# Casting and subtracting streamed weights two k-tiles at a time, with two S5 phase tables in a shared buffer

## The chip, the cores and the metric

The kernel runs on one core of one Trainium2 chip. The metric is device time in microseconds (us); three timed runs of a version give a median. The core's engines named below are PE (TensorE, the matmuls), PEld (the weight load of PE), DVE (VectorE), ACT (ScalarE) and SP (SyncE, which issues most of the loads). Each engine takes its instructions in a fixed order, and they wait for one another by semaphores.

## What is computed

The reference is one pre-norm layer of a hybrid encoder on 256 tokens of 2048 channels, in float32. Cut to what matters here:

```python
h = rmsnorm(x, norm_mix_g)
proj = h @ w_in                        # 2048 x 12288
lru_x, lru_gate, q, k, v, ssm_u, gates = split(proj)
y_a = rg_lru_branch(lru_x, lru_gate, ...)
y_b = chunk_attention_branch(q, k, v, rel_bias)
y_c = gelu(s5_branch(ssm_u, ...))      # complex diagonal state space
br_a, br_b = y_a @ w_branch[0], y_b @ w_branch[1]
br_c = (y_c @ w_branch[2]) * sigmoid(y_c @ ssm_w_glu)
g = sigmoid(gates + gate_bias)
x = x + (g[0] * br_a + g[1] * br_b + g[2] * br_c) @ w_out
h = rmsnorm(x, norm_ffn_g)
x = x + (silu(h @ w_ffn_gate) * (h @ w_ffn_up)) @ w_ffn_down   # hidden 5632
out = rmsnorm(x, norm_final_g)
```

The S5 branch turns each state by an angle per token: `lb = mag * (cos(ang) + i sin(ang))`. The kernel runs the recurrence with real factors `mag` and multiplies by tables of cosine and sine before and after it; the argument of these tables is the phase that the change speaks of.

## The kernel before

**Weight stream.** Every large matrix is cut into columns of 512 and rows of 128 (a k-tile). `add_job` (L161) queues a block of 512 columns as steps of `UK = 2` k-tiles; a step is called a unit here. `load_unit` (L166) brings a unit into a `raw` tile of 2 x 512 columns by one DMA from SP (L170; the first two units use two DMAs, L175), and then, k-tile by k-tile, calls `split` (L120): ACT casts the raw weights to fp32r into `hi` (L123), DVE subtracts `hi` from the raw weights into `lo` (L124). There are 3 `raw` buffers (of a unit each) and `HBUF = 7` buffers each of `hi` and `lo` (of a k-tile each). A `raw` buffer is free for the next DMA when its two subtractions are done; a `hi` or `lo` buffer is free for the next k-tile when its matmuls are done. The last 512 columns are special: eight units are cast into large tiles that stay (`resident`, L908, through `place`, L916).

**Matmuls.** The tokens, split in the same way, are the stationary operand, the weights move. `as_body` (L185) does three matmuls per k-tile and half of the tokens: high by `hi` (L198), high by `lo` (L199), low by `hi` (L200). That makes 12 matmuls per unit, which add up in PSUM until the block's last unit; then `evac` takes the sum out.

**Order.** `run_steps` (L209) writes out the steps; loads and splits are written `LOOK` = 2 units ahead and with a raised priority. Behind each step the generators of the three mixers (`gen_lru`, `gen_att`, `gen_s5`) get a share of instructions (`bg_mix`, L772). A scheduler that simulates a timeline then fixes the order of instructions on each engine, under these priorities and the buffers that are free. So a changed length or buffer can change the order of anything.

**Stages.** Mixer projections, gates and branch products come first, with the mixers' own arithmetic beside them; `drain("s5")` and `gen_yc` (L757) stand before the first product of the S5 output. Then the output projection, the FFN in two parts, and the last 512 columns with the final norm (`last_body`, L944; `finish`, L920).

**S5 phase tables.** `gen_s5` works through 8 blocks of channels with two halves each (`sb`, L696). For each half, `q` and `w` (L698, L699, one buffer each, tags `sq` and `sw`) are filled: `q` on ACT (L702), `w` and again `q` on DVE (L703, L704), `w` on ACT (L705). Sine of `q` and cosine of `w` (L706, L707) make the tables `sn` and `cs_`, which have one buffer each too. The products with the matmul results (L720 to L723) go into `ma` and `mb` (L717, tags `sA` and `sB`, one buffer each); sums, scans and further products follow, and L738 is the last to read `mb`. The matmuls L745 and L746 read `ma`, and L748 puts their result into `u`.

Of the kernel before, what the change touches and what calls it, by code (L numbers as in the profile page):

```python
# [10 lines left out]
F32 = mybir.dt.float32  # L11
F32R = mybir.dt.float32r
# [6 lines left out]
P = 128  # L19
S = 256  # L20
D = 2048
# [10 lines left out]
HBUF = 7  # L32
# [13 lines left out]
# columns of the constant array  # L46
# [8 lines left out]
# rows of the per-channel parameter block  # L55
# [5 lines left out]
def trunk(  # L61
# [21 lines left out]
    # ---------------------------------------------------------------- inputs  # L83
# [6 lines left out]
    # the tensor engine's clock rises while the first loads are under way  # L90
# [17 lines left out]
    def load_params():  # L108
        act.dma_start(cst[:, P:], consts[:, P:])
        prm_r = const.tile([P, P], F32, name="prm_r")  # L110
        act.dma_start(prm_r[R_G2:R_G2 + 16], norm_ffn_g[0].rearrange("(k p) -> k p", p=P))
        act.dma_start(prm_r[R_CW:R_CW + 32], lru_conv_w[0].rearrange("c (k p) -> (c k) p", p=P))
        for r0, src in ((R_CB, lru_conv_b), (R_BA, lru_ba), (R_BX, lru_bx), (R_LAM, lru_lambda), (R_D, ssm_d)):
            act.dma_start(prm_r[r0:r0 + 8], src[0].rearrange("(k p) -> k p", p=P))
        tps = sm("prm_ps")
        pe.transpose(tps[:, :R_N], prm_r[:R_N, :], ident[:R_N, :R_N])
        vec.tensor_copy(prm, tps[:, :R_N])

    # ---------------------------------------------------------------- helpers
    def split(dst_hi, dst_lo, src, scale=None):  # L120
        """src (optionally scaled per partition) as an exact sum of two f32r parts"""
        if scale is None:
            act.copy(dst_hi, src)  # L123
            vec.tensor_sub(dst_lo, src, dst_hi.bitcast(F32))  # L124
        else:
            act.activation(dst_hi, src, AF.Identity, scale=scale)
            vec.scalar_tensor_tensor(dst_lo, src, scale, dst_hi.bitcast(F32), ALU.mult, ALU.subtract)

    def rstd_of(dst, ss, scr):
        """dst = (ss / D + EPS) ** -0.5 on [P, 2] tiles, refined by a Newton step"""  # L130
        v, t = scr[:, 0:2], scr[:, 2:4]
        vec.tensor_scalar(v, ss, 1.0 / D, EPS, ALU.mult, ALU.add)
        act.activation(t, v, AF.Sqrt)
        vec.reciprocal(dst, t)
        vec.tensor_mul(t, dst, dst)
        vec.tensor_mul(t, t, v)
        vec.tensor_scalar(t, t, -0.5, 1.5, ALU.mult, ALU.add)
        vec.tensor_mul(dst, dst, t)

    def expacc(dst, src, pool, tag):  # L140
        """dst = exp(src) in float32 accuracy"""
# [16 lines left out]
    # ---------------------------------------------------------------- main stream of weight units  # L158
    steps = []

    def add_job(src, kt, c0, body, pre=None):  # L161
        """columns c0..c0+512 of a [kt * 128, n] matrix, UK k-tiles at a time"""
        for k0 in range(0, kt, UK):
            steps.append((src, k0, c0, body, kt, pre if k0 == 0 else None))

    def load_unit(st, idx):  # L166
        src, k0, c0, _, _, _ = st
        raw = wp.tile([P, UK, 512], F32, tag="raw", name="raw", bufs=3)
        if idx > 1:
            nc.sync.dma_start(  # L170
                raw, src[k0 * P:(k0 + UK) * P, c0:c0 + 512].rearrange("(k p) n -> p k n", p=P))
        parts = []
        for kk in range(UK):
            if idx <= 1:
                nc.sync.dma_start(raw[:, kk, :], src[(k0 + kk) * P:(k0 + kk + 1) * P, c0:c0 + 512])  # L175
            if idx in place:
                hi, lo = place[idx](kk)
            else:
                hi = wp.tile([P, 512], F32R, tag="hi", name="hi", bufs=HBUF)
                lo = wp.tile([P, 512], F32R, tag="lo", name="lo", bufs=HBUF)  # L180
            split(hi, lo, raw[:, kk, :])
            parts.append((hi, lo))
        return parts

    def as_body(get_x, evac):  # L185
        """out tiles: tokens stationary, weights moving"""
# [22 lines left out]
    def run_steps(bg, budget):  # L209
        """emits every queued step; background work fills in behind each"""  # L210
# [21 lines left out]
    # ---------------------------------------------------------------- x^T and its norm  # L232
# [3 lines left out]
    def transpose_tokens(src, kt0, name):  # L236
        """two 128-column tiles of token-major src, transposed into one PSUM bank [P, 2, S]"""
        t = sm(name)
        for i in range(2):
            for h in range(2):  # L240
                pe.transpose(t[:, i * S + h * P:i * S + (h + 1) * P], src(h, kt0 + i), ident)  # L241
        return t
# [31 lines left out]
    # ---------------------------------------------------------------- projections of the mixers  # L274
    # token-major input of the S5, replaced by its feature-major output block by block
# [8 lines left out]
    def fm_evac(name, dst):  # L284
        """scales by rstd and transposes; dst(m) is the place of feature tiles m, m + 1"""
# [21 lines left out]
    # RG-LRU  # L307
# [18 lines left out]
    # gates  # L326
# [69 lines left out]
    # attention  # L396
# [26 lines left out]
    # ---------------------------------------------------------------- background: RG-LRU  # L423
    def gen_lru():
        # softplus(-lambda)
# [20 lines left out]
        for hf in range(2):  # L446
# [40 lines left out]
            # t1 = tanh(L / 2), t3 = 1 / (1 + t1) refined; t1 := -(1 - a) / 2  # L487
# [26 lines left out]
    # ---------------------------------------------------------------- background: attention  # L514
# [72 lines left out]
    # ---------------------------------------------------------------- background: S5  # L587
    def gen_s5():
        # per-state parameters, state = 128 * j + partition
# [20 lines left out]
        # f = angle / (2 pi), reduced to [-0.5, 0.5]  # L610
# [42 lines left out]
        for b in range(8):  # L653
# [18 lines left out]
            # partitions 32 * jj.. hold the channels of state tile 4 * b + jj: B (re, im), then u, as hi and lo  # L672
# [8 lines left out]
            # stationaries [B_hi; B_hi; B_lo] and moving parts [u_hi; u_lo; u_hi], 32 channels each  # L681
# [14 lines left out]
            for sb in range(2):  # L696
                j0 = 4 * b + 2 * sb
                q = mx.tile([P, 2, S], F32, tag="sq", name="sq")  # L698
                w = mx.tile([P, 2, S], F32, tag="sw", name="sw")  # L699
# [72 lines left out]
    def bg_mix(budget):  # L772
        """spends the budget of a unit on background steps; a negative cost ends the generator's turn"""
# [41 lines left out]
    # ---------------------------------------------------------------- output projection  # L815
# [30 lines left out]
    # ---------------------------------------------------------------- FFN  # L846
# [53 lines left out]
    # ---------------------------------------------------------------- last columns and the final norm  # L900
    # the weights of the last 512 columns stay on chip, so that the first 128 tokens finish early
# [6 lines left out]
    def resident(i, kk):  # L908
        q = i // n_res
        if i % n_res == 0 and kk == 0:  # L910
            pool, tags = ((big, ("TH", "TL")), (fp, ("h2h", "h2l")))[q]
            held.append(tuple(pool.tile([P, 8, 512], F32R, tag=t, name="res") for t in tags))
        return tuple(t[:, (i % n_res) * UK + kk, :] for t in held[q])

    for i in range(2 * n_res):
        place[base + i] = lambda kk, i=i: resident(i, kk)  # L916
# [86 lines left out]
```

## Time and profile before

| what | value |
|---|---|
| timed runs | 1636.93, 1636.76, 1635.12 us, median 1636.76 us |
| profiled execution, from its first to its last instruction | 1637.8 us (the page gives no other time for it) |
| PE / DVE / ACT busy, share of the span | 98% / 68% / 58% |
| casts `hi<-raw` (L123) | 1088 of 128x512, 621 ns mean |
| subtractions `lo<-raw,hi` (L124) | 1088 of 128x512, 688 ns mean |
| unit loads of 512 KB | median 3.7 to 4.7 us from issue to landing, by matrix |
| HBM rate over the span | 185 GB/s |

The busy time of PE counts overlapping matmuls as one stretch, and the end of a matmul is modelled, so 98% says that PE seldom stood empty, not that each matmul came as early as it could. The distance from one matmul's start to the next one's tells the latter. A row of the timeline gives the start, the duration, the engine, the line, the operation, output and inputs, the number of instructions merged into the row, and in square brackets the idle time before it with what ended it.

### The profile page before, as it was taken

To read this page: it belongs to the slowest core of one execution; us is meant where nothing else is said; L and a number is where in the kernel's file an instruction comes from. 1 tells how busy PE (TensorE), PEld (TensorE's weight loads), DVE (VectorE), ACT (ScalarE), POOL (GpSimd) and SP (SyncE) were. 2 spreads that over 40 slices of the span, in tenths; PEclk is the share of its full clock that TensorE was granted. 3 is DMA by queue.
4 is the path that set the end of the run, shared out by engine and by line. 5 is a ranking of instruction groups with operands and counts; after the bars stand their busy time and mean duration, and the time that the engine had idled before them with its cause. 6 is when DMAs were issued, how large, how long until landed. Compare 5 with 4: busy or idle time off the path is not lost.

```text
span 1637.8 us, 21032 instructions
## 1 busy us (share of the span) xinstructions
PE 1612.1 (98%) x7263; PEld 1307.1 (80%) x7263; DVE 1111.4 (68%) x1910; ACT 951.6 (58%) x1696; POOL 0.8 (0%) x6
## 2 busy tenths in 40 slices
PE   7999999999999999999999999999999999999997
PEld 4877877778888777778888888888888888888886
DVE  4869889879697978876666555555555555555654
ACT  4677677675768676665455554555444455455443
POOL 0000000000000000000000000000000000000000
PEclk9999999999999999999999999999999999999999
DMA  8665566655554646565666666666666666666564
GB/s 224 198 178 150 166 183 185 186 165 174 165 177 146 197 152 214 170 201 185 214 236 182 193 191 190 185 192 190 187 192 196 193 187 194 190 192 186 188 191 144
DMA packets 169933, 304.21 MB, mean 186 GB/s; under 512 B 22185, under 2 KB 26721, under 8 KB 169057
## 3 DMA queue, kind: packets, MB, share of 16 engines
q1 hardware_dynamic: 153104, 292.66, 59.5%
q10 hardware_dynamic: 16720, 10.20, 2.3%
q8 instruction: 57, 0.93, 0.2%
q14 instruction: 52, 0.42, 0.1%
HBM read 300.71 MB, written 2.11 MB: 185 GB/s over the span
## 4 chain that ended last, share of the span: by engine, by line
PE 86%; DVE 5%; ACT 3%; DMA 3%; issue 2%; ACTq 0%; DVEq 0%
PE mm L199 27%; PE mm L200 27%; PE mm L198 27%; DMA raw<-in_w_in 3%; DVE lo L124 2%; ACT hi L123 1%; PE y_ps L746 1%; PE mm L957 1%; PE at_ps L241 1%; PE mm L956 1%; PE mm L958 1%; PE y_ps L745 0%; ACT bc L691 0%; DVE xc L470 0%; ACT bc L692 0%
## 5 line engine op out<-in xcount | busy, mean ns | idle before, releaser
L124 DVE TENSOR_TENSOR lo<-raw,hi 128x512 fp32r<-128x512 f32 x1088 | 736.9, 688 | 441.6 <-ACT hi L123 438.9
L123 ACT CAST hi<-raw 128x512 fp32r<-128x512 f32 x1088 | 658.7, 621 | 611.9 <-DVE lo L124 322.2
L199 PE MATMUL mm<-lo,xth 128*128 128x512 f32 x768 | 304.8, 397 | 2.6 <-DVE lo L124 2.6
L200 PE MATMUL mm<-hi,xtl 128*128 128x512 f32 x768 | 302.7, 394 | 0.0
L198 PE MATMUL mm<-hi,xth 128*128 128x512 f32 x768 | 284.2, 396 | 9.6 <-ACT hi L123 9.6
L200 PE MATMUL mm<-hi,h2l 128*128 128x512 f32 x704 | 275.0, 391 | 0.0
L198 PE MATMUL mm<-hi,h2h 128*128 128x512 f32 x704 | 274.9, 390 | 0.0
L199 PE MATMUL mm<-lo,h2h 128*128 128x512 f32 x704 | 274.0, 389 | 0.0
L198 PEld LDWEIGHTS mm<-hi,xth 128*128 128x128 f32 x768 | 144.0, 189 | 46.5 <-ACT hi L123 13.7
L199 PEld LDWEIGHTS mm<-lo,xth 128*128 128x128 f32 x768 | 145.0, 189 | 39.5 <-DVE lo L124 8.3
L200 PEld LDWEIGHTS mm<-hi,xtl 128*128 128x128 f32 x768 | 145.2, 189 | 29.4 <-issue 0.4
L199 PEld LDWEIGHTS mm<-lo,h2h 128*128 128x128 f32 x704 | 132.2, 188 | 27.3
L200 PEld LDWEIGHTS mm<-hi,h2l 128*128 128x128 f32 x704 | 132.1, 188 | 27.2
L198 PEld LDWEIGHTS mm<-hi,h2h 128*128 128x128 f32 x704 | 132.2, 188 | 26.8
L198 PE MATMUL mm<-hi,at 128*128 128x512 f32 x312 | 121.6, 390 | 0.0
L200 PE MATMUL mm<-hi,at 128*128 128x512 f32 x312 | 121.6, 390 | 0.0
L199 PE MATMUL mm<-lo,at 128*128 128x512 f32 x312 | 121.4, 389 | 0.0
L199 PEld LDWEIGHTS mm<-lo,at 128*128 128x128 f32 x312 | 58.6, 188 | 12.2
L200 PEld LDWEIGHTS mm<-hi,at 128*128 128x128 f32 x312 | 58.6, 188 | 12.2
L198 PEld LDWEIGHTS mm<-hi,at 128*128 128x128 f32 x312 | 58.6, 188 | 11.9
L200 PE MATMUL mm<-hi,mtl 128*128 128x512 f32 x128 | 50.3, 393 | 0.0
L199 PE MATMUL mm<-lo,yc 128*128 128x512 f32 x128 | 50.1, 391 | 0.0
(312 smaller groups left out, 1624.7 us busy)
## 6 DMA issues: line engine op xcount, KB each, us to landing
raw<-in_w_in SPq DMA_DIRECT2D x190, 512.0 KB, 4.2
raw<-in_w_ffn_gate SPq DMA_DIRECT2D x88, 512.0 KB, 4.0
raw<-in_w_ffn_up SPq DMA_DIRECT2D x88, 512.0 KB, 3.7
raw<-in_w_ffn_down SPq DMA_DIRECT2D x88, 512.0 KB, 4.7
raw<-in_w_branch SPq DMA_DIRECT2D x48, 512.0 KB, 4.1
raw<-in_w_out SPq DMA_DIRECT2D x32, 512.0 KB, 4.6
raw<-in_ssm_w_glu SPq DMA_DIRECT2D x16, 512.0 KB, 4.7
xa<-in_x SPq DMA_DIRECT2D x8, 256.0 KB, 3.8
```

What stands on the lines that cost most here:

```text
L123: act.copy(dst_hi, src)
L124: vec.tensor_sub(dst_lo, src, dst_hi.bitcast(F32))
L198: pe.matmul(acc[h], xh[:, k, hs], hi, start=k == 0, stop=False)
L199: pe.matmul(acc[h], xh[:, k, hs], lo, start=False, stop=False)
L200: pe.matmul(acc[h], xl[:, k, hs], hi, start=False, stop=k == kt - 1)
L241: pe.transpose(t[:, i * S + h * P:i * S + (h + 1) * P], src(h, kt0 + i), ident)
L746: pe.matmul(yp[rs, :S], ct[:, 1, rs], m2[:, i, :], start=False, stop=True)
L956: pe.matmul(last_acc[h], ah[:, k, hs], hi, start=k == 0, stop=False)
L957: pe.matmul(last_acc[h], ah[:, k, hs], lo, start=False, stop=False)
L958: pe.matmul(last_acc[h], al[:, k, hs], hi, start=False, stop=k == kt - 1)
```

## The change

It makes the unit the grain of the split as well as of the load. `hi` and `lo` become tiles of 2 x 512 columns with four buffers each, so that eight k-tiles of each part have room in place of seven, given back two at a time. From the third unit on, one cast and one subtraction on 1024 columns take the place of two and two on 512; the first two units are still loaded and split by k-tile. The resident tiles of the last columns are handed out by unit, and are split in the same way. The matmuls, their order in a step and the loads are as before.

The room for the eighth k-tile comes from the S5: `q` and `w` are now the two halves of one tile `qw` that has the tag `sB`, that is, the single buffer in which `mb` lies. In program order that buffer goes to `qw` of a half, then to `mb` of that half, then to `qw` of the next half; each must wait until the last reader of the one before is done.

The raw block of per-channel parameters, `prm_r` (L110), moves from a buffer of its own into the S5's tag `uf` (a tile that each S5 block fills at L677 and reads at L748). It is loaded at the start and transposed once (L116); the profile has that transpose at 35.5 us and the first use of `uf` by the S5 at 82.7 us.

The rest of the diff takes out comments and is left out.

```diff
-HBUF = 7
+HBUF = 4
...
-        prm_r = const.tile([P, P], F32, name="prm_r")
+        prm_r = mx.tile([P, S], F32, tag="uf", name="prm_r")[:, :P]
...
     def load_unit(st, idx):
         src, k0, c0, _, _, _ = st
         raw = wp.tile([P, UK, 512], F32, tag="raw", name="raw", bufs=3)
+        if idx in place:
+            hi, lo = place[idx]()
+        else:
+            hi = wp.tile([P, UK, 512], F32R, tag="hi", name="hi", bufs=HBUF)
+            lo = wp.tile([P, UK, 512], F32R, tag="lo", name="lo", bufs=HBUF)
         if idx > 1:
             nc.sync.dma_start(
                 raw, src[k0 * P:(k0 + UK) * P, c0:c0 + 512].rearrange("(k p) n -> p k n", p=P))
-        parts = []
-        for kk in range(UK):
-            if idx <= 1:
+            split(hi, lo, raw)
+        else:
+            for kk in range(UK):
                 nc.sync.dma_start(raw[:, kk, :], src[(k0 + kk) * P:(k0 + kk + 1) * P, c0:c0 + 512])
-            if idx in place:
-                hi, lo = place[idx](kk)
-            else:
-                hi = wp.tile([P, 512], F32R, tag="hi", name="hi", bufs=HBUF)
-                lo = wp.tile([P, 512], F32R, tag="lo", name="lo", bufs=HBUF)
-            split(hi, lo, raw[:, kk, :])
-            parts.append((hi, lo))
-        return parts
+                split(hi[:, kk, :], lo[:, kk, :], raw[:, kk, :])
+        return [(hi[:, kk, :], lo[:, kk, :]) for kk in range(UK)]
...
             for sb in range(2):
                 j0 = 4 * b + 2 * sb
-                q = mx.tile([P, 2, S], F32, tag="sq", name="sq")
-                w = mx.tile([P, 2, S], F32, tag="sw", name="sw")
+                qw = mx.tile([P, 2, 2, S], F32, tag="sB", name="qw")
+                q, w = qw[:, 0], qw[:, 1]
...
-    def resident(i, kk):
+    def resident(i):
         q = i // n_res
-        if i % n_res == 0 and kk == 0:
+        if i % n_res == 0:
             pool, tags = ((big, ("TH", "TL")), (fp, ("h2h", "h2l")))[q]
             held.append(tuple(pool.tile([P, 8, 512], F32R, tag=t, name="res") for t in tags))
-        return tuple(t[:, (i % n_res) * UK + kk, :] for t in held[q])
+        return tuple(t[:, (i % n_res) * UK:(i % n_res + 1) * UK, :] for t in held[q])
 
     for i in range(2 * n_res):
-        place[base + i] = lambda kk, i=i: resident(i, kk)
+        place[base + i] = lambda i=i: resident(i)
```

## The prediction

> **What bounds the kernel now.** I read the page first (busy time, chain, groups), then stretches of the span, then the timeline.
>
> ```profile
> span 1637.8 us, 21032 instructions
> ...
> PE 1612.1 (98%) x7263; PEld 1307.1 (80%) x7263; DVE 1111.4 (68%) x1910; ACT 951.6 (58%) x1696; POOL 0.8 (0%) x6
> ...
> PE 86%; DVE 5%; ACT 3%; DMA 3%; issue 2%; ACTq 0%; DVEq 0%
> ...
> L124 DVE TENSOR_TENSOR lo<-raw,hi 128x512 fp32r<-128x512 f32 x1088 | 736.9, 688 | 441.6 <-ACT hi L123 438.9
> L123 ACT CAST hi<-raw 128x512 fp32r<-128x512 f32 x1088 | 658.7, 621 | 611.9 <-DVE lo L124 322.2
> ```
>
> PE holds 86% of the chain that ended last. The two groups that the change merges fill most of ACT and DVE, but these engines are the bound only where PE stands waiting for them. The stretches show where (busy us and instructions of PE, PEld, DVE, ACT and POOL, then clock, DMA share, GB/s):
>
> ```profile
> 0.00:46.00 46.00, 34.66 (x134) 23.50 (x135) 24.29 (x80) 22.95 (x47) 0.76 (x6) 0.89 0.83 214
> 94.00:310.00 216.00, 211.62 (x949) 167.29 (x948) 185.52 (x310) 155.11 (x280) 0.00 (x0) 1.00 0.59 175
> 310.00:717.00 407.00, 406.19 (x1875) 322.69 (x1875) 343.99 (x609) 278.32 (x529) 0.00 (x0) 1.00 0.59 176
> 717.00:1611.00 894.00, 894.00 (x4019) 740.27 (x4018) 514.93 (x780) 451.84 (x757) 0.00 (x0) 1.00 0.64 195
> ```
>
> From 717 us on PE has no idle time at all. Whether it also runs at its pace there, the timeline tells:
>
> ```profile
> 999.71 0.39 PE L198 MATMUL mm<-hi,h2h 128*128 128x512 f32 x1
> ...
> 1005.83 0.39 PE L198 MATMUL mm<-hi,h2h 128*128 128x512 f32 x1
> ```
> ```profile
> 1000.59 0.62 ACT L123 CAST hi<-raw 128x512 fp32r<-128x512 f32 x1 [0.74 <-DVE lo L124]
> 1001.25 0.69 DVE L124 TENSOR_TENSOR lo<-raw,hi 128x512 fp32r<-128x512 f32 x1 [0.67 <-ACT hi L123]
> 1001.95 0.62 ACT L123 CAST hi<-raw 128x512 fp32r<-128x512 f32 x1 [0.74 <-DVE lo L124]
> ```
>
> Between the two PE rows lie 27 equal steps: 6.12 / 27 = 0.227 us per matmul, 2.72 us per unit of 12. ACT and DVE look like a ping-pong of 1.36 us per k-tile, but 1.36 is also six matmuls, and no cast depends on the subtraction just before it. A cast waits for a buffer that PE frees; the subtraction merely ends 0.01 us earlier and gets the name. So the 322 us under that name aren't to be won.
>
> What PE does lose to the stream lies before 717 us:
>
> ```profile
> PEld mm L198 <- ACT hi L123: 7.2, 11, 1.3
> PEld mm L199 <- DVE lo L124: 5.6, 11, 1.3
> ```
> ```profile
> PE mm L198 <- ACT hi L123: 7.5, 5, 2.3
> ```
>
> The first two rows are the waits in 94 to 717 us (total, times, longest): 12.8 us. The third is PE before 94 us. These some 20 us are all that faster casts and subtractions could give back.
>
> **The merged instructions.** The trace already has the wide forms, on the S5 output, and pairs of the narrow ones:
>
> ```profile
> L123 ACT CAST yc<-u 128x1024 fp32r<-128x1024 f32 x2 | 2.0, 1048 | 0.0
> L124 DVE TENSOR_TENSOR yc<-u,yc 128x1024 fp32r<-128x1024 f32 x2 | 2.4, 1223 | 0.2 <-ACT yc L123 0.2
> ```
> ```profile
> 704.99 1.14 ACT L123 CAST hi<-raw 128x512 fp32r<-128x512 f32 x2 [1.17 <-DMA raw<-in_w_in]
> 709.89 1.29 DVE L124 TENSOR_TENSOR lo<-raw,hi 128x512 fp32r<-128x512 f32 x2 [2.33 <-ACT hi L123]
> 711.37 2.36 DVE L124 TENSOR_TENSOR yc<-u,yc 128x1024 fp32r<-128x1024 f32 x2 [0.18 <-ACT yc L123]
> ```
>
> By means, a unit saves 2 x 0.62 - 1.05 = 0.19 us of ACT and 2 x 0.69 - 1.22 = 0.15 us of DVE. But neighbours overlap: a pair costs 1.14 and 1.29, so where the engine is full, which alone matters, the gain is 0.09 and 0.07 us. The Trainium skill (VectorE: DVE Perf Modes, "The DRAIN you can't avoid") has the next operation start only when the pipe is empty, unless nothing holds it; by that the gain would be the 0.15. The pair of 1.29, under 2 x 0.69, speaks for the smaller figure.
>
> What it costs is latency. `hi` of a unit's first k-tile comes 1.05 - 0.62 = 0.43 us later, `lo` (1.05 + 1.22) - (0.62 + 0.69) = 0.96 us later.
>
> **From 717 to 1611 us: nothing.** A unit's buffer comes free; cast and subtraction take 2.3 us, PE reads the result three units (8.2 us) later. The raw buffer is free 2.3 us after that start too; with a landing of 4.7 us,
>
> ```profile
> raw<-in_w_ffn_down SPq DMA_DIRECT2D x88, 512.0 KB, 4.7
> ```
>
> it is full again at 7.0 of 8.2 us. This cover of 1.2 us hides the stage; were it gone, its 328 units would cost what is missing in each. SP's loads keep their order and number.
>
> **From 94 to 717 us: -2 us.** 12.8 us of waits are the most to win. Against it, 11 waits for `hi` and 11 for `lo` could each grow by 0.43 and 0.96, 15 us at worst. DVE is busy 185.5 of 216 us at 94 to 310 us; 0.07 us in each of about 75 units is 5 us of relief there. I take -2, between -8 and +6.
>
> **The start: +2 us.** Here ACT was held by issuing a load for 5.3 us, and PE ran dry:
>
> ```profile
> 20.82 5.27 ACTq L597 DMA_DIRECT2D s5b<-in_ssm_b_im  x1
> ```
> ```profile
> 26.80 0.73 PE L198 MATMUL mm<-hi,xth 128*128 128x512 f32 x2 [2.19 <-ACT hi L123]
> ...
> 30.12 0.63 PE L200 MATMUL mm<-hi,xtl 128*128 128x512 f32 x1
> 30.55 0.63 PE L199 MATMUL mm<-lo,xth 128*128 128x512 f32 x1
> ...
> 32.61 0.74 PE L198 MATMUL mm<-hi,xth 128*128 128x512 f32 x2 [0.49 <-ACT hi L123]
> ...
> 38.54 1.22 PE L198 MATMUL mm<-hi,xth 128*128 128x512 f32 x2 [2.26 <-ACT hi L123]
> 41.09 0.80 PE L199 MATMUL mm<-lo,xth 128*128 128x512 f32 x1 [1.33 <-DVE lo L124]
> ```
>
> PE starts dry three times (26.80, 32.61, 38.54), so up to 3 x 0.96 = 2.9 us more; below zero, -2.2, if the new order moves a cast ahead of that issue. I take +2. After the first dry spell matmuls start 0.43 apart (30.12 to 30.55) in place of 0.227: a half clock. The Trainium skill (TensorE: Matmul & The Clock Gate, "Part 1: The HAM clock gate") halves the clock after an idle window of about 3.4 us. The row shows it after 2.19 us of idle, so the measurement decides and shorter gaps count too. By the rule none of these gaps, lengthened by 0.96, would cost a clock by itself; by the rows each may.
>
> `prm_r` in the buffer of `uf`: nothing, since it is transposed long before the S5 needs the buffer (both times stand with the change); it would cost only if the S5's start were ready before the parameters.
>
> **The S5 tables: 0 us, with a risk.** Before, `q` and `w` of the next half are made as soon as the last sine has been taken. Now they wait for L738, and this chain stands before L720:
>
> ```profile
> L702 ACT ACTIVATE sq<-cst,s5par x32: 492/496/512, 58.5 to 641.5; 128x256 f32<-128x256 f32 x32
> L703 DVE TENSOR_SCALAR sw<-sq x16: 406/426/428, 59.4 to 642.7; 128x512 f32<-128x512 f32 x16
> L704 DVE SCALAR_TENSOR_TENSOR sq<-sw,sq x16: 672/684/693, 60.0 to 644.4; 128x512 f32<-128x512 f32 x16
> L705 ACT ACTIVATE sw<-sq x16: 622/628/635, 60.8 to 645.9; 128x512 f32<-128x512 f32 x16
> ```
> ```profile
> 678.15 0.69 DVE L738 TENSOR_TENSOR sA<-sA,sB 128x512 f32<-128x512 f32 x1
> ...
> 679.22 0.72 ACT L707 ACTIVATE tab<-sw,cst 128x512 f32<-128x512 f32 x1
> ...
> 685.59 0.67 DVE L720 TENSOR_TENSOR sA<-tab,bu_re 128x512 f32<-128x512 f32 x1
> ```
>
> Two L702 (0.99), L703 (0.43), L704 (0.68), L705 (0.63), L707 (0.72): 3.45 us. The old chain from the end of L738 (678.84) through L745 and L746, which must read `ma` first, to L720 takes 6.75 us and covers it. Each of three changes of engine may stand behind one wide cast or subtraction (up to 1.22): 3.45 to 7.1 us, so 0 to 0.4 us on the path. L703 and L704 now wait at the head of DVE's queue, with the next subtraction behind them, and PE behind that once its units in hand are used up.
>
> **The end: +1 us.** The last unit arrives just in time:
>
> ```profile
> 1612.68 1.14 ACT L123 CAST hi<-raw 128x512 fp32r<-128x512 f32 x2 [0.89 <-DMA raw<-in_w_ffn_down]
> ...
> 1614.08 0.50 PE L957 MATMUL mm<-lo,at 128*128 128x512 f32 x1
> ```
>
> `lo` comes 0.96 us later; PE can fill in with the other half of the tokens, so 0 to 2 us, and I take 1.
>
> **Sum.** -2 + 2 + 0 + 1 = +1 on the span of 1637.8. The runs' median is 1636.76, 1.0 below it: 1637.8 as a time, say 1638.
>
> **Rivals.**
> 1. *Slower: the S5 ends too late.* The last block's split ends at 713.7 (711.37 + 2.36); PE needs it at
>
> ```profile
> 717.73 0.39 PE L198 MATMUL mm<-hi,yc 128*128 128x512 f32 x1
> ```
>
> 4.0 us later. If the scheduler sets the table chain behind the old one instead of beside it, a half loses 3.45 us and a table load of 1.28: 4.7. If only the last three blocks' second halves add up, 14.1 - 4.0 = 10 us at that place: 1648. It decides from a delay of 4.0 us on. For it: the S5 is a serial chain there. Against: the 6.75 us of cover.
> 2. *Faster: the waits go.* If the relief on DVE and ACT takes 8 of the 12.8 us and the start gains nothing or little: 1636.8 - 8 + 1 = 1630. For it: DVE at 86% at 94 to 310 us. Against: 0.07 us per unit is little.
> 3. *Slower: a worse start.* Three waits grow by 2.9 us and one more half-clock spell of some ten matmuls costs 10 x 0.2 = 2.0; with 1 at the end, 1636.8 + 5.9 = 1643. For it: PE starts dry already. Against: one cast and one subtraction less to wait for in each unit.
> 4. *No wide form.* The instructions stay two by two, nothing is saved or delayed: 1637. For it: the wide forms shown are of other tiles. Against: raw, `hi` and `lo` of a unit each lie in one piece.
>
> **How the numbers follow.** About 0.2%, 3.3 us, is what a measurement of this kernel can tell from no change: 1633.5 to 1640. Forecast (inside these bounds) 0.46, rivals 0.20, 0.20, 0.10, 0.04. Faster 0.20; same 0.46 + 0.04 = 0.50; slower 0.30. The range takes in rivals 1 to 3: 1629 to 1649.
>
> **What would show it.** Right: about 550 wide casts near 1.05 us and subtractions near 1.22, matmuls 0.227 apart from 717 us on, and the first matmul on `yc` without a wait. Wrong: PE idle before `yc` (rival 1), PE's waits for `hi` and `lo` in 94 to 717 us near 4 or over 20 us, more half clock before 94 us, or PE idle after 717 us, where the cover of 1.2 us would have failed.

## The result, and the profile after

The changed kernel takes 1655.94 us (median of four runs, 1650.87 to 1656.73), the kernel before 1635.94 us (four runs). The ratio is 1.0111, with a 95% interval of 1.0094 to 1.0129: slower by some 18 us, outside the predicted range of 1629 to 1649.

In the code of the changed kernel the lines behind the weight stream stand one lower than before: its matmuls are L197 to L199, and the last sum of an S5 half is L737 (L738 before). The page of its profiled execution has the span, the busy times, and the two merged groups:

```profile
span 1653.5 us, 19462 instructions
...
PE 1618.9 (98%) x7263; PEld 1312.5 (79%) x7263; DVE 1049.3 (63%) x1360; ACT 872.3 (53%) x1149; POOL 0.8 (0%) x6
...
L124 DVE TENSOR_TENSOR lo<-raw,hi 128x1024 fp32r<-128x1024 f32 (+1 forms) x546 | 663.8, 1217 | 507.3 <-ACT hi L123 505.6
L123 ACT CAST hi<-raw 128x1024 fp32r<-128x1024 f32 (+1 forms) x546 | 571.6, 1050 | 673.6 <-PE mm L199 496.4
```

The instructions have merged as announced, at 1217 and 1050 ns. DVE is busy 62 us less than before and ACT 79 us less, and the kernel is 16 us longer by its span. The stretches say where (columns as before):

```profile
94.00:310.00 216.00, 208.96 (x928) 164.47 (x926) 174.28 (x233) 148.50 (x213) 0.00 (x0) 0.99 0.55 170
310.00:731.00 421.00, 417.39 (x1907) 331.86 (x1908) 342.43 (x486) 269.59 (x403) 0.00 (x0) 0.99 0.57 174
731.00:1613.00 882.00, 882.00 (x3969) 731.75 (x3968) 459.72 (x444) 385.78 (x423) 0.00 (x0) 1.00 0.61 193
```

From 731 us on PE has no idle time, as before from 717. Most of what is lost is lost ahead of that: in 94 to 310 us PE gets through 928 instructions where it got through 949, while DVE is busy 11 us less there.

The first matmul on each stationary operand cuts the span into stretches that hold the same products of the weight stream in every version, but for a dozen at most; of PE's other matmuls up to 14 fall on the other side of a border (times in us between those first matmuls, from the traces):

| version | first on xth | xth to ya | ya to yb | yb to yc | yc to res | res to end | span |
|---|---|---|---|---|---|---|---|
| before | 8.7 | 261.6 | 302.4 | 145.0 | 882.9 | 37.2 | 1637.8 |
| changed | 9.3 | 266.6 | 309.2 | 146.1 | 882.2 | 40.1 | 1653.5 |

The loss is 0.6 + 5.0 + 6.8 + 1.1 - 0.7 + 2.9 = 15.7 us, the difference of the spans. Finer steps show when stream matmuls of the same number are compared, at places where PE has also done as many others. By the clock of the kernel before, the changed kernel is 1.8 us behind at 93 us, level at 162, 5.5 behind at 190, 6.9 at 300, 10.6 at 316, 11.1 at 555 and 13.5 at 691 us. Two views of the changed kernel tell what PE did there. First the waits of PE's weight loads in 94 to 745 us (total, times, longest), then one wait of DVE in the same stretch:

```profile
PEld mm L198 <- DVE lo L124: 11.0, 11, 2.4
PEld mm L197 <- ACT hi L123: 5.5, 7, 1.6
```
```profile
DVE bt L535 <- DMA bt<-rb_scratch: 8.0, 2, 7.0
```

The waits for `lo` have gone from 5.6 to 11.0 us. But 16.5 us in place of 12.8 is not 13 us more, so the timeline of a single dry spell is worth a look. DVE's rows, then PE's:

```profile
301.42 1.28 DVE L368 SCALAR_TENSOR_TENSOR merged<-merged,mm 128x512 f32<-128x512 f32 x2
309.71 0.27 DVE L535 MEMSET bt<- 64x256 f32 x1 [7.01 <-DMA bt<-rb_scratch]
309.90 2.28 DVE L124 TENSOR_TENSOR lo<-raw,hi 128x1024 fp32r<-128x1024 f32 x2
```
```profile
309.16 0.28 PE L711 MATMUL bu_im<-bc 96*128 96x256 f32 x1
311.11 0.80 PE L198 MATMUL mm<-lo,ya 128*128 128x512 f32 x1 [1.67 <-DVE lo L124]
311.71 0.63 PE L199 MATMUL mm<-hi,ya 128*128 128x512 f32 x1
312.13 0.63 PE L198 MATMUL mm<-lo,ya 128*128 128x512 f32 x1
312.56 0.63 PE L199 MATMUL mm<-hi,ya 128*128 128x512 f32 x1
```

A memset of 0.27 us on the attention's bias tile stands 7.0 us at the head of DVE's queue, because it waits for a DMA. Two subtractions stand behind it, PE runs dry for 1.67 us, and the matmuls after that start 0.43 us apart in place of 0.227: a half clock. There are more such spells (1.6, 2.18 and 2.39 us from start to start at 137, 187 and 601 us). To add them up, take each distance between two starts on PE against the median distance for the same two lines. From xth to res, those more than 0.32 us over it sum to 25.1 us (before 14.4), and those 0.12 to 0.32 us over it, most of them the half clock, to 10.8 (before 6.2). Smaller deviations sum to 9.0 (before 11.7). That is 10.7 + 4.6 - 2.7 = 12.6 us more, and the stretches give 5.0 + 6.8 + 1.1 - 0.7 = 12.2.

One of the changed kernel's places shows the moved tables at work. ACT's rows, LRU gates (L478 to L485) and the phase tables (L704 to L706) between two casts:

```profile
149.67 1.05 ACT L123 CAST hi<-raw 128x1024 fp32r<-128x1024 f32 x1 [0.35 <-DMA raw<-in_w_in]
150.74 1.28 ACT L484 ACT_TABLE_LOAD   x1
152.04 0.60 ACT L484 ACTIVATE lt<-lt,lp 128x256 f32<-128x256 f32 x1
152.55 0.61 ACT L704 ACTIVATE qw<-qw 128x512 f32<-128x512 f32 x1
153.18 1.28 ACT L705 ACT_TABLE_LOAD   x1
...
155.12 1.28 ACT L485 ACT_TABLE_LOAD   x1
...
157.04 1.28 ACT L706 ACT_TABLE_LOAD   x1
...
159.07 1.28 ACT L478 ACT_TABLE_LOAD   x1
...
161.10 1.05 ACT L123 CAST hi<-raw 128x1024 fp32r<-128x1024 f32 x1
```

Sine and LRU gates take turns, each turn pays a function-table load, and 11.4 us lie between two casts. DVE stands for 9.0 us of it. PE had units in hand, so that only 1.9 us of this show on PE, between 162 and 176 us. What follows costs more. In the kernel before and in the version with wide instructions and own tables below, the sine of the same half (the third of S5) starts at 141.4 and 139.6 us, ahead of the gates; here at 154.5, among them. The scan of the LRU then starts at 182.05 us in place of 174.13, and at 187 us PE runs dry again. DVE's rows, then PE's:

```profile
182.05 2.28 DVE L505 TENSOR_TENSOR_SCAN lt<-lt 128x1024 f32<-128x1024 f32 x1
...
186.72 1.22 DVE L506 TENSOR_TENSOR lt<-lt,gt 128x1024 f32<-128x1024 f32 x1
187.86 1.22 DVE L124 TENSOR_TENSOR lo<-raw,hi 128x1024 fp32r<-128x1024 f32 x1
```
```profile
186.73 0.61 PE L197 MATMUL mm<-hi,xth 128*128 128x512 f32 x2
189.13 0.50 PE L198 MATMUL mm<-lo,xth 128*128 128x512 f32 x1 [1.79 <-DVE lo L124]
```

With the half clock behind it this spell sets PE back by 3.7 us. From 170 to 190 us DVE and ACT have LRU and gate instructions beside the weights, and none of the S5: if the shared buffer is at work here, it is by the LRU that it made late.

### The profile page after: what moved, and what is told of

The parts are those of the page before. It is cut to its first block, busy times and chain, and to the rows that moved or that the text cites. A ratio compares the mean times of both kernels' runs of the same rounds, so it can differ in the third digit from the quotient of the medians.

```text
span 1653.5 us, 19462 instructions
## 1 busy us (share of the span) xinstructions
PE 1618.9 (98%) x7263; PEld 1312.5 (79%) x7263; DVE 1049.3 (63%) x1360; ACT 872.3 (53%) x1149; POOL 0.8 (0%) x6
## 4 chain that ended last, share of the span: by engine, by line
PE 79%; DVE 7%; ACT 6%; DMA 4%; issue 3%; ACTq 1%; SPq 0%; DVEq 0%
PE mm L198 25%; PE mm L199 25%; PE mm L197 25%; DVE lo L124 2%; ACT hi L123 1%; DMA raw<-in_w_in 1%; DMA raw<-in_w_ffn_down 1%; DMA raw<-in_w_branch 1%; ACT bc L690 1%; PE y_ps L745 1%; PE at_ps L240 1%; ACT bc L688 1%; ACT bc L691 1%; DMA xa<-in_x 0%; DMA bd<-in_lru_wa 0%
## 5 line engine op out<-in xcount | busy, mean ns | idle before, releaser
L124 DVE TENSOR_TENSOR lo<-raw,hi 128x1024 fp32r<-128x1024 f32 (+1 forms) x546 | 663.8, 1217 | 507.3 <-ACT hi L123 505.6
L123 ACT CAST hi<-raw 128x1024 fp32r<-128x1024 f32 (+1 forms) x546 | 571.6, 1050 | 673.6 <-PE mm L199 496.4
L199 PE MATMUL mm<-hi,xtl 128*128 128x512 f32 x768 | 304.0, 396 | 0.0
L197 PE MATMUL mm<-hi,xth 128*128 128x512 f32 x768 | 292.5, 397 | 9.9 <-ACT hi L123 9.9
L197 PE MATMUL mm<-hi,h2h 128*128 128x512 f32 x704 | 274.9, 390 | 0.0
L199 PE MATMUL mm<-hi,h2l 128*128 128x512 f32 x704 | 274.0, 389 | 0.0
L197 PEld LDWEIGHTS mm<-hi,xth 128*128 128x128 f32 x768 | 144.8, 190 | 44.0 <-ACT hi L123 13.0
L198 PEld LDWEIGHTS mm<-lo,xth 128*128 128x128 f32 x768 | 145.6, 190 | 42.3 <-DVE lo L124 10.8
L199 PEld LDWEIGHTS mm<-hi,xtl 128*128 128x128 f32 x768 | 145.6, 190 | 33.5 <-issue 4.5
L197 PEld LDWEIGHTS mm<-hi,h2h 128*128 128x128 f32 x704 | 132.2, 188 | 27.1
L199 PEld LDWEIGHTS mm<-hi,h2l 128*128 128x128 f32 x704 | 132.2, 188 | 27.0
L197 PE MATMUL mm<-hi,at 128*128 128x512 f32 x312 | 121.6, 390 | 0.0
L199 PE MATMUL mm<-hi,at 128*128 128x512 f32 x312 | 121.4, 389 | 0.0
L197 PEld LDWEIGHTS mm<-hi,at 128*128 128x128 f32 x312 | 58.6, 188 | 12.2
L199 PEld LDWEIGHTS mm<-hi,at 128*128 128x128 f32 x312 | 58.6, 188 | 11.9
L199 PE MATMUL mm<-hi,yc 128*128 128x512 f32 x128 | 50.1, 391 | 0.0
L199 PE MATMUL mm<-hi,mtl 128*128 128x512 f32 x128 | 50.0, 391 | 0.0
```

The source lines that it names most:

```text
L197: pe.matmul(acc[h], xh[:, k, hs], hi, start=k == 0, stop=False)
L198: pe.matmul(acc[h], xh[:, k, hs], lo, start=False, stop=False)
L199: pe.matmul(acc[h], xl[:, k, hs], hi, start=False, stop=k == kt - 1)
```

## The experiments

No version leaves out a part of the computation. Ratios are to the kernel before, run on the same chip beside them. "First matmul" figures are as in the table above.

### Each part by itself

**Tables alone.** The kernel before, with `q` and `w` in the buffer `sB`:

```diff
-                q = mx.tile([P, 2, S], F32, tag="sq", name="sq")
-                w = mx.tile([P, 2, S], F32, tag="sw", name="sw")
+                qw = mx.tile([P, 2, 2, S], F32, tag="sB", name="qw")
+                q, w = qw[:, 0], qw[:, 1]
```

> The kernel before, with the shared S5 table buffer alone (narrow instructions, seven k-tile buffers). Theory W (the wide instructions let PE run dry): 1636 us, within 3 of before, no dry spell of PE over 2 us after 94 us. Theory T (the shared table buffer delays the S5 and through it the stream): 1648 to 1656 us, with PE waiting over 1.5 us for lo near 190, 310 or 600 us. Theory O (any new order of the scheduler does it): somewhere from 1636 to 1655 us.

1661.28 us, ratio 1.0143 (1.0126 to 1.0160): the shared buffer alone costs no less than the whole change. Its stretch from yb to yc takes 159.9 us in place of 145.0, with a wait of 8.8 us for `yc`.

**The changed kernel without wide instructions.**

```diff
-            split(hi, lo, raw)
+            for kk in range(UK):
+                split(hi[:, kk, :], lo[:, kk, :], raw[:, kk, :])
```

> The changed kernel (four unit buffers, shared tables), but each unit is cast and subtracted k-tile by k-tile. Theory W: 1636 to 1640 us, since the wide instructions are gone. Theory T, and a theory B that the four unit buffers, given back in pairs, are at fault: 1648 to 1656 us. Theory O: anywhere between.

1664.33 us, 1.0161 (1.0146 to 1.0176), slower than the changed kernel. The stretch from yb to yc takes 166.4 us. PE's weight loads in 700 to 745 us show why (its lines there are numbered as in the kernel before):

```profile
PEld y_ps L745 <- issue: 8.4, 1, 8.4
PEld mm L198 <- ACT yc L123: 4.5, 1, 4.5
```

PE stands for the last S5 matmuls and then for `yc`. S5's chain between two halves, DVE's rows and ACT's:

```profile
711.81 0.69 DVE L738 TENSOR_TENSOR sA<-sA,sB 128x512 f32<-128x512 f32 x1
...
713.85 0.43 DVE L703 TENSOR_SCALAR qw<-qw 128x512 f32<-128x512 f32 x1
...
715.14 0.69 DVE L704 SCALAR_TENSOR_TENSOR qw<-qw 128x512 f32<-128x512 f32 x1
...
720.08 0.69 DVE L722 TENSOR_TENSOR sA<-tab,bu_im 128x512 f32<-128x512 f32 x1 [1.33 <-ACT tab L706]
```
```profile
712.92 0.90 ACT L702 ACTIVATE qw<-cst,s5par 128x256 f32<-128x256 f32 x2
713.88 1.14 ACT L123 CAST hi<-raw 128x512 fp32r<-128x512 f32 x2
716.42 1.14 ACT L123 CAST hi<-raw 128x512 fp32r<-128x512 f32 x2 [1.40 <-DMA raw<-in_w_in]
717.47 0.63 ACT L705 ACTIVATE qw<-qw 128x512 f32<-128x512 f32 x1
718.12 1.28 ACT L706 ACT_TABLE_LOAD   x1
719.41 0.64 ACT L706 ACTIVATE tab<-qw 128x512 f32<-128x512 f32 x1
```

From the end of L738 (712.50) to the first product (720.08) lie 7.6 us, and the last thing that DVE waits for is the table. On the way the chain stands behind a cast that itself waits 1.40 us for a weight load, and it pays a table load of 1.28 us. In the kernel before the same two points lie 6.75 us apart at this half, so this place explains 0.8 us. S5's last L738 starts at 735.2 us in place of 701.2, and the section on the prediction comes back to the rest.

**Wide instructions with own tables, three unit buffers** (no room for a fourth):

```diff
-HBUF = 4
+HBUF = 3
...
-                qw = mx.tile([P, 2, 2, S], F32, tag="sB", name="qw")
-                q, w = qw[:, 0], qw[:, 1]
+                q = mx.tile([P, 2, S], F32, tag="sq", name="sq")
+                w = mx.tile([P, 2, S], F32, tag="sw", name="sw")
```

> The changed kernel with wide instructions, but the tables in two buffers of their own as before; for lack of room three unit buffers of hi and lo in place of four. Theory W: 1650 to 1662 us (three unit buffers can only make it worse). Theory T: 1637 to 1642 us. Theory O: anywhere between.

1662.82 us, 1.0153 (1.0131 to 1.0176). It loses 12.2 us between ya and yb alone (314.6 against 302.4). PE's waits for `hi` and `lo` in 94 to 740 us are 24.8 us. That run changes the number of buffers along with the tables, so it says nothing of the tables.

**Wide instructions only from unit 256 on**, after the mixers, and not in the resident units; the changed kernel otherwise:

```diff
-            split(hi, lo, raw)
+            if idx >= 256 and idx not in place:
+                split(hi, lo, raw)
+            else:
+                for kk in range(UK):
+                    split(hi[:, kk, :], lo[:, kk, :], raw[:, kk, :])
```

> The changed kernel with wide instructions only from the output projection on (unit 256 and later, without the resident last columns); the mixer stage is narrow. Theory W: 1636 to 1640 us, no loss after 717 us, and no dry spells before. Theories T and B: 1648 to 1654 us. If the wide instructions cost time in the FFN as well, over 1640 us with PE idle after 717 us.

1665.35 us, 1.0172 (1.0152 to 1.0191): as slow as all narrow. From yc to res it takes 884.4 us, all narrow 884.8. So wide instructions in the FFN neither gain nor cost that these runs can tell.

### Two factors, taken apart

The own tables and four paired unit buffers fit together if the attention scores get one buffer instead of two. That gives the missing corners.

**Wide, own tables:** the changed kernel with

```diff
-                s = mx.tile([P, 2, 384], F32, tag="s", name="s", bufs=2)
+                s = mx.tile([P, 2, 384], F32, tag="s", name="s", bufs=1)
...
-        rows = mx.tile([32, 3, P], F32, tag="s", name="s5rows", bufs=2)
+        rows = mx.tile([32, 3, P], F32, tag="s", name="s5rows", bufs=1)
...
-                qw = mx.tile([P, 2, 2, S], F32, tag="sB", name="qw")
-                q, w = qw[:, 0], qw[:, 1]
+                q = mx.tile([P, 2, S], F32, tag="sq", name="sq")
+                w = mx.tile([P, 2, S], F32, tag="sw", name="sw")
```

> The changed kernel with the phase tables in buffers of their own again (the room comes from one buffer instead of two for the attention scores). Wide instructions and four paired unit buffers are left. Theory T (the shared table buffer is the main cost, the wide instructions win some 8 us where it is there): 1628 to 1640 us, yc with slack ahead of yb's end, S5's last add before 708 us. Theory W+B (wide units in pairs let PE run dry, whatever the tables do): 1648 to 1660, with stalls of over 1 us and half clock before 700 us. Theory O (any new order costs some 15 to 20 us against a lucky one): 1650 to 1665.

**Narrow, own tables:** the same, with the two-line loop of the second experiment in place of `split(hi, lo, raw)`.

> The run before this one, with each k-tile's cast and subtraction made by themselves (512 columns), into the same four paired buffers: only the pairing of the buffers and their number differ from the kernel before. Theory T: 1634 to 1642. Theory B (pairs that are freed together cost): 1645 or more. Theory O: 1650 to 1665.

1644.46 us, 1.0027 (1.0017 to 1.0037) for wide; 1637.62 us, 0.9992 (0.9981 to 1.0002) for narrow. S5's last L738 (L737 in the wide one) is back at 703.5 and 701.5 us. These two differ from the other corners in the scores' buffer too; the tables alone, above, show the cost of sharing without that.

Would another order of the instructions have told another story? All four corners were run again with a budget for the background of 1.55 per step, which changes the order all over:

```diff
-BUDGET = 1.45
+BUDGET = 1.55
```

> Narrow instructions, four paired buffers, own tables, and the background's budget per step 1.55 in place of 1.45 (all four runs of this set have it): S5's parts are then planned 13 steps of weight units earlier, some 36 us by the rate of 224 steps in 620 us. Theory T (the shared buffer makes S5 late for yc): own tables had no such lateness, so about the same as at 1.45, 1634 to 1642. Theory O (the order's luck alone decides): anywhere from 1635 to 1660.

> Wide instructions, own tables, budget 1.55. Theory W (wide units cost some 7 us by dry spells of PE behind a late lo, whatever the plan): 5 to 9 us over the run before this one. Theory O: the difference has another sign or size (under 2 us or over 12).

> The changed kernel with budget 1.55 and nothing else. Theory T as lateness: S5 now has some 36 us in hand, so the shared buffer costs little, 1640 to 1650 (within 4 us of wide with own tables). Theory T as dispatch (the chain's instructions stand at the head of ACT's and DVE's queues and hold up casts): it still costs 8 us or more over own tables, 1652 to 1665. Theory O: no pattern.

> Narrow instructions, four paired buffers, shared tables, budget 1.55. At 1.45 this gave 1664, with two waits for yc of 8.4 and 4.2 us. Theory T as lateness: the waits for yc are gone, 1638 to 1648. Theory T as dispatch: 1652 to 1665 with dry spells before 700 us. Theory O: no pattern.

The ratios of all eight, with their intervals:

| budget | tables | narrow | wide |
|---|---|---|---|
| 1.45 | own | 0.9992 (0.9981 to 1.0002) | 1.0027 (1.0017 to 1.0037) |
| 1.45 | shared | 1.0161 (1.0146 to 1.0176) | 1.0111 (1.0094 to 1.0129) |
| 1.55 | own | 1.0010 (1.0001 to 1.0019) | 1.0032 (1.0021 to 1.0044) |
| 1.55 | shared | 1.0139 (1.0122 to 1.0156) | 1.0084 (1.0067 to 1.0101) |

The pattern holds in both orders. Sharing costs 1.7 and 1.3% with narrow instructions, 0.8 and 0.5% with wide ones. Wide instructions cost 0.35 and 0.2% with own tables and win 0.5% with shared ones. Luck of the order as the main cause of this pattern is out.

What failed in these expectations is the lever: the larger budget brought S5 forward only in the middle. With narrow instructions and own tables its L738 starts 31 us earlier at the ninth half (434.4 against 465.2) and level with 1.45 at the thirteenth (609.5), and the last stands at 700.6 us (701.5 at 1.45). With shared tables the last stands at 726.4, and PE still waits 8.6 us for `yc`. What takes the lead away again isn't settled; it is not S5's own chain alone, which would have kept it.

### Other numbers of buffers

**Eight single buffers per part**, the kernel before otherwise:

```diff
-HBUF = 7
+HBUF = 8
```

with the attention scores in one buffer and `prm_r` in `uf` for the room (so three things change);

> The kernel before with eight k-tile buffers per part in place of seven (the same bytes as four pairs; one buffer fewer for the attention scores, and the parameter rows in the uf buffer, to make room). No wide instruction, no shared tables, no pairs. Theories T, W and B: 1632 to 1640, since one more buffer can only help. Theory O (the planned order changes and with it the luck): 1645 to 1665.

and **six**, with `HBUF = 6` as the only edit:

> The kernel before with six k-tile buffers per part in place of seven: another neutral change of the order. T, W and B: 1636 to 1644 (PE waits for hi and lo may rise some us before 717 us; the FFN has room). Theory O: 1650 to 1665.

1652.92 us, 1.0077 (1.0051 to 1.0103), and 1660.85 us, 1.0134 (1.0115 to 1.0153). One buffer more was expected to help and cost 13 us. At 302 to 309 us it has the same picture as the changed kernel, in DVE's rows:

```profile
307.21 0.27 DVE L536 MEMSET bt<- 64x256 f32 x1 [7.97 <-DMA bt<-rb_scratch]
307.41 3.02 DVE L124 TENSOR_TENSOR lo<-raw,hi 128x512 fp32r<-128x512 f32 x5
```

PE's distance from start to start is 4.56 us there. With six buffers the waits of PE's weight loads for `hi` and `lo` in 94 to 745 us are 33.3 us, against 12.8 with seven; one wait of 7.2 us stands behind the memset, which stood 5.6 us there. The rest says that six k-tiles are too few, in three pairs or singly. Both versions have tables of their own, and yet S5's last L738 starts at 716.4 and 718.5 us: the shared buffer is not the only thing that makes S5 late.

### The memset at the head of DVE's queue

Three versions with the memset on POOL, whose queue has nothing else to do:

```diff
-            vec.memset(bt[0:64, 0, :, 0:64], MASK)
+            nc.gpsimd.memset(bt[0:64, 0, :, 0:64], MASK)
```

In wide with own tables, and in the eight single buffers, the orders of PE and ACT stay as good as the same.

> Wide instructions with own tables (1644.5), and the memset of the attention bias tile issued by POOL instead of DVE; the orders of PE and ACT are the same, DVE's differs by the two memsets. There DVE's queue stood 7.9 us at that memset and PE ran dry for 3.17 us behind it. Theory H (an instruction that waits for a DMA at the head of DVE's queue is what a wide unit makes visible): the dry spell (2.9 us over the regular 0.23) and its eight half-clock matmuls (8 x 0.2 = 1.6) go, 1639 to 1641, no gap over 1 us between 290 and 310. Theory W (the wide instructions themselves are late): 1643 to 1646, the gap stays.

> Eight single buffers (1652.9) with the memset on POOL; the order of PE and ACT is as good as the same. Theory H: the gap of 4.56 us at 303.5 and its half clock go, 1645 to 1648; the wait for yc of 4.2 us near 724 gets longer or stays, since S5 isn't moved. Theory O (order alone): 1651 to 1655.

> The changed kernel with the memset of the bias tile on POOL. The 7.0 us of DVE at 302 to 309 go. Theory H: the gap of 1.95 us at 309 and its half clock go, and with it 3 to 4 us: 1651 to 1653. If the shared tables' lateness then becomes what ends last at yc (S5's end at 715 against yb's end at 731): no less than 1650. Theory W: 1654 to 1657.

Wide with own tables: 1638.62 us, 0.9992 (0.9982 to 1.0003), that is 5.8 us less. Eight buffers: 1647.30 us, 1.0044 (1.0028 to 1.0061), 5.6 us less. In the profiles the stretch from ya to yb gets shorter by 6.0 and 5.6 us, and no other changes by more than 1.4. What else the eight buffers cost is open, but for a wait of 2.7 us for `yc`. DVE's rows of wide with own tables, at first with the memset on DVE, then with it on POOL:

```profile
300.79 0.27 DVE L535 MEMSET bt<- 64x256 f32 x1 [7.88 <-DMA bt<-rb_scratch]
300.99 3.42 DVE L124 TENSOR_TENSOR lo<-raw,hi 128x1024 fp32r<-128x1024 f32 x3
```
```profile
292.95 1.37 DVE L368 SCALAR_TENSOR_TENSOR merged<-merged,mm 128x512 f32<-128x512 f32 x2 [1.58 <-PE mm L199]
298.78 3.50 DVE L124 TENSOR_TENSOR lo<-raw,hi 128x1024 fp32r<-128x1024 f32 x3 [4.47 <-ACT hi L123]
```

Three subtractions in a row start 2.2 us sooner, and PE no longer runs dry there: the gap of 3.17 us at 299 and its half clock are gone.

In the changed kernel itself the same edit gained nothing: 1658.74 us, 1.0115 (1.0094 to 1.0136). There the order of PE and DVE changed in many places. Up to the first matmul on yb it is 7.2 us ahead of the changed kernel (577.9 against 585.1), but 14 of the S5's instructions on PE stand behind that border instead of ahead of it; at equal work it is 4.6 us ahead, 3.3 of it won at the memset. Between yb and yc it loses this and 2.2 us more. Its S5 has the last L737 at 718.4 us, in place of 709.5. How much of the loss is the new order is not separated.

The control, **the kernel before with the memset on POOL** and nothing else:

> The kernel before with the memset of the bias tile on POOL and nothing else: the orders of PE and ACT stay the same. There DVE stood 3.3 us in two times at that memset and PE showed no gap over 1 us behind it. Theory H (the memset's wait costs only where it stands so long that PE runs dry): within 1.5 us of the kernel before. That POOL's memset saves time by itself: 3 us or more faster, which would mean that the 5.9 us saved in the wide kernel with own tables say nothing of wide instructions.

1639.04 us, 1.0003 (0.9993 to 1.0012): no gain where DVE stood 2.2 us at most. This pair also shows how far one profiled execution can be trusted: the order of PE and ACT is the same, and yet xth to ya, ahead of the memset, takes 258.7 us in place of 261.6. A difference of some 3 us in one stretch of one execution says little.

### Sharing with something outside the loop

**Narrow, tables in the two buffers of the attention scores:** the narrow version with own tables, with the scores' two buffers restored and

```diff
-                q = mx.tile([P, 2, S], F32, tag="sq", name="sq")
-                w = mx.tile([P, 2, S], F32, tag="sw", name="sw")
+                q = mx.tile([P, 2, S], F32, tag="s", name="sq", bufs=2)
+                w = mx.tile([P, 2, S], F32, tag="s", name="sw", bufs=2)
```

> Narrow instructions, four paired buffers, and the phase tables in the two buffers of the attention scores (which are used for four short stretches) in place of the buffer of S5's own products: shared, but with something outside S5's chain. Theory T as a loop (the next half's tables must wait for this half's last product, as in the run that gave 1664): the loop is gone, S5's last add before 708 us, 1636 to 1643. Theory that any shared buffer delays S5 by as much: 1655 or more, with waits for yc.

1649.73 us, 1.0061 (1.0046 to 1.0076), between the two theories, and PE waits for `yc`:

```profile
PEld mm L198 <- ACT yc L123: 7.0, 1, 7.0
```

The starts of L738, from the traces, say where the time went; the comparison is the narrow version with own tables. At the eighth of the sixteen halves S5 is level (405.3 against 406.0 us). While the attention uses the scores, from about 400 to 515 us, it falls behind, and at the eleventh half it is 14.4 us late (557.7 against 543.3). From there to the last half it takes 157.1 us, against 158.2. With `sB` shared (the narrow version at the top) S5 is 13.2 us late at the eighth half, 23.6 at the eleventh and 33.7 at the last. This fits a shared buffer that costs S5 time while its other user holds it; `sB` is held by S5 itself in every half. The order of the instructions changed as well.

### The end

**Wide with own tables, memset on POOL, resident units narrow:**

```diff
-            split(hi, lo, raw)
+            if idx in place:
+                for kk in range(UK):
+                    split(hi[:, kk, :], lo[:, kk, :], raw[:, kk, :])
+            else:
+                split(hi, lo, raw)
```

> Wide instructions in the stream with own tables and the memset on POOL (1638.6), and the resident last units cast k-tile by k-tile again. The wide tail cost about 2 us (39.6 us from the first res matmul to the end, against 37.2 before): theory W in the tail, 1636 to 1638, with no more than 38.5 us from the first res matmul to the end. If the tail's cost has another source: 1638 to 1640, the tail as long.

1639.66 us, 1.0003 (0.9994 to 1.0013); from the first res matmul to the end 39.5 us, with the wide resident units 39.6. The wide casts of the last units are not what makes the end longer. None of the versions is measurably faster than the kernel before.

## Why the prediction was wrong

It gave +1 us as the sum of four steps; measured on the spans it is +15.7: 1.8 up to 93 us, 11.7 from there to the first matmul on yc, -0.7 to that on res, and 2.9 to the end.

**From 717 to 1611 us: nothing.** Right. From yc to res PE takes 882.2 us in place of 882.9. The saving of 0.07 us (DVE) and 0.09 us (ACT) per unit was right too. Narrow against wide with own tables, DVE's busy time falls from 1086.5 to 1050.0 us and ACT's from 916.6 to 865.6, of which two table loads fewer are 2.6. By 550 merged units that is 0.066 and 0.088 us, not the 0.15 and 0.19 of the means. (The other 25 of the 62 us that DVE is busy less than before are there with narrow instructions too.) It is worth nothing where PE is the bound.

**The S5 tables: 0 us, with a risk.** This is the step that failed. The term measured 9.8 us by the spans in the changed kernel (with shared tables against own ones), and added alone to the kernel before it cost 1.4%, some 23 us. The step priced one path only, from one half's L738 to the next half's first product within a block, and there it wasn't far off. Narrow with shared against narrow with own tables, the eight stretches of this kind sum to 54.6 us against 50.9. (Its sum of 3.45 us left out the sine of 0.64 and the table load of 1.28 that the rows above show ahead of the product.) The loop is real: with own tables both tables are ready 4.5 to 7.2 us before the first product that reads them, with shared ones that product starts within 0.9 us of a table's end, in all eight.

But S5's last L738 comes 33.7 us later, and most of that lies where the step did not look. The seven changes from block to block take 274.6 us against 252.3, and the products themselves, from the first product of a half to L738, 310.0 against 302.6. At a change of block the tables are ready in time (at the thirteenth half at 609.0 us, the first product at 619.7); PE's matmul on the new block's input ends last (617.9). What changed is that the tables, which were made a turn ahead, are now made in the same stretch as the new block's own casts, on the same ACT and DVE. That this is what lengthens it is likely, not tested; a part is the stream itself, which is late there too.

Rival 1 named the lateness and its place, PE idle before `yc`, and with narrow instructions that is what happened. It took 14.1 us of lateness from the second halves of the last three blocks, at 4.7 each. S5 does fall 17.0 us behind the kernel before in the last three blocks, but only 6.3 of these in the second halves, and 17.0 more come ahead of these blocks: rival 1 had the place and not the account.

In the changed kernel itself PE did not wait for `yc`. Its S5 was 8 us later than before (709.5 against 701.2), and PE was later than S5. There the shared buffer costs 0.84% over wide with own tables, or 9.8 us between the two spans. At equal work 8.3 of these are there by the first matmul on ya, and 8.6 at 555 us. Late tables among the LRU gates, and the late LRU behind them, are what the trace shows there, as in the rows above. The run has 35 table loads, wide with own tables 30 and the kernel before 32. Which share of the 10 us they cause was not tried.

**From 94 to 717 us: -2 us, between -8 and +6.** Measured from 93 us to the first matmul on yc, +11.7, most of it the tables' as just said. Wide instructions with own tables lose 3.7 us there, within the bounds. Even so the account was short. The bounds counted waits as they stood and let each grow by the longer latency. They left out that a subtraction waits behind whatever waits ahead of it on DVE. A memset that stood 2.2 us at most in the kernel before stood 7 to 8 us in the three versions shown, and with wide units two or three subtractions of 1.2 us pile up behind it. At the budget of 1.45 that wait, with the half clock after it, accounts for the whole cost of the wide instructions with own tables: 1.0027 with it, 0.9992 without. At 1.55, where it stood 5.4 us, that was not tried. The prediction looked for what stands behind a waiting instruction only at the two that the change moved.

**The start: +2 us.** About right: the first matmul on xth is 0.6 us later, and at 93 us the stream is 1.8 us behind. With the noise of one stretch that may be luck.

**The end: +1 us.** It measured +2.9. The cause given, `lo` of a wide unit being later, fell: narrow resident units changed nothing. Other versions lie between 37.4 and 42.6 us there, the kernel before with nothing but its memset moved at 38.8. Those with a narrow stream all lie at 38.8 or below, those with a wide one between 38.2 and 42.6; what sets it is open.

Rival 2's relief of DVE is real in one case. With shared tables, wide instructions bring S5's last L738 from 735.2 to 709.5 us and win 0.5%. Why 0.07 us per unit moves S5 by 26 us isn't settled; it gains 5 to 7 us in each of the last four blocks.

## What to carry to other kernels

A small buffer is free to share only if its next writer doesn't have to wait for the loop's own last reader; otherwise work that was made one turn ahead becomes part of the loop, and falls among other work on every engine that it passes. Price it at every such place, not only on the path from the last reader to the next use. Before a change that makes an engine's instructions longer, look for the instructions on it that wait for a DMA: the longer ones pile up behind them. And test two factors in all four corners, with a second order of the instructions: here wide instructions cost by themselves and win beside a worse fault.

## What the runs showed of the hardware

After a pause of PE of 1.67 us, behind a few short S5 matmuls, the rows from 311.71 us on start 0.43 us apart: a half clock. In the prediction's row the pause was 2.19 us, at 187 us above 1.79. Not every such pause has it: in the changed kernel without wide instructions PE stands 1.71 us before 91.46 us, and the matmuls behind it go on 0.23 apart.

A function-table load costs ACT 1.28 us and no more that the rows show: after the one at 150.74 us the next instruction starts at 152.04. The Trainium skill (ScalarE: Activation LUTs, "What ACT_TABLE_LOAD costs") gives about 1283 ns for the load and 1380 ns more for a drain. The first agrees with the trace; the second has no room between these rows, nor ahead of the load, as the cast before it ends at 150.72.
